# Expert inputs fetched as rows by an indirect DMA instead of computed as one-hot products

## The chip, the cores and the metric

The kernel runs on one core of a Trainium2 chip. The metric is the device time of one execution in microseconds (us). A core has TensorE (PE in the profile; its weight loads are PEld), VectorE (DVE), ScalarE (ACT), GpSimd (POOL) and SyncE (SP), each with an instruction queue of its own that runs in order, and 16 DMA engines that all queues share. SP issues nearly all transfers here; POOL can issue them too, and is the engine that issues an indirect one, whose source addresses come from a table of indices.

## The reference, cut to what matters

A two-layer decoder trunk on 256 tokens of width 1024, float32. The last sub-layer, which takes more than half of the time, is a mixture of 8 SwiGLU experts of which each token uses two:

```python
logits = (ht @ router)                       # 256 x 8
top_logit, top_idx = lax.top_k(logits, 2)
top_w = jax.nn.softmax(top_logit, axis=-1)
xb = h_pad[row_tok]                          # the tokens of an expert, as rows
...
gt, up = jnp.split(xe @ w_gu[e], 2, axis=-1) # w_gu[e]: 1024 x 7168
yb = (jax.nn.silu(gt) * up) @ w_down[e]      # w_down[e]: 3584 x 1024
out = zeros.at[row_tok].add(yb * row_w)
```

512 assignments go to 8 experts, 64 each on average, not all equal. What an expert needs as its input is a selection of the 256 rows of `h`, with the model dimension on the partitions, since that is what TensorE contracts over.

## The kernel before, in words

An expert is worked on in 128 slots. `rank` gives each token its slot in each expert. `slots` (line 1965) makes the one-hot matrix `P` (two tiles of 128 tokens x 128 slots) by comparing `rank` with an iota on DVE. `slots_t` (1973) transposes `P` on PE into `PT`, which later carries the expert's output back to the tokens (`back`, 2055). `disp` (1979) makes the expert's input: for each of eight 128-wide pieces of the model dimension, two float32 products of a piece of `hn` (the 256 rows of `h`, kept in SBUF) with `P` give the piece of the selected rows, already transposed, in PSUM. `disp_out` (1986) splits it into a high and a low float32r part: `xeh` by ACT, `xel` by DVE. `part` (1991) is one third of that: 0 makes and transposes `P`, 1 and 2 make four pieces each.

The weights of all eight experts are streamed once. `wstream` (456) loads tiles of 1 MB (or two halves) into twelve rotating `raw` buffers; of each 512 KB ACT makes the high part (`whi<-raw`) and DVE the low part (`wlo<-raw,whi`), in four rotating pairs, and `mm3` (448) issues three float32r products for each 512 columns: high x high, high x low, low x high. An expert has seven column blocks j. For each, `run_experts` (2184) issues the gate (8 x 3 products of 512 columns), the down projection of the block before (24) and the up projection (24). The next expert's `part`s are hung into the up projection of block 4, behind its products k = 1, 4 and 7 (lines 2197 to 2199).

Up to the routing the order on the engines is set by the kernel's own list of tasks (`spin`). In the expert loop the framework orders the instructions when the kernel is built; for the first experts it keeps the order in which they are written, and from the middle on it interleaves them. A few weight tiles go to buffers that are later used for something else (`raw_once`, 2231), among them `lnbb`, which in the end holds the last layer norm's bias, loaded by `ln_rows` (1484) from `moe_hook` (2219).

SP issues a load when its buffer has been released by DVE. It runs its instructions in order, so a transfer that waits holds back the loads behind it.

Of the kernel before, what the change touches and what calls it, by code (L numbers as in the profile page):

```python
# [24 lines left out]
F32 = mybir.dt.float32  # L25
F32R = mybir.dt.float32r
I32 = mybir.dt.int32
# [5 lines left out]
D = 1024  # L33
S = 256
DFF = 2816
NE = 8
# [4 lines left out]
LNX_EPS = 64e-5  # L41
RANK0 = 1000
NEG = -1.0e30
CW = 1029


def _consts():
    p = np.arange(128)[:, None]
    j = np.arange(128)[None, :]
    c = np.zeros((128, CW), np.float32)  # L50
    c[:, 0:128] = p == j
    c[:, 128:256] = p < j
    c[:, 256:384] = j - RANK0
    c[:, 384:512] = (p <= j) & (p // 64 == j // 64)
    t = j % 64
    s = p % 64
    c[:, 512:640] = np.where(j < 64, s < t, s <= t)
    q = np.arange(64)[None, :]
    c[:, 640:704] = (q % 2 == 1) & (s == q - 1)
    for i, b in enumerate((2, 4, 8, 16)):  # L60
        c[:, 704 + 64 * i:768 + 64 * i] = ((q // b) % 2 == 1) & (s // b == q // b - 1)
    c[:, 960:1024] = s == q
    c[:, 1024] = np.arange(128) == 63
    c[:, 1025] = np.arange(128) == 127
    s = s[:, 0]
    c[:, 1026] = -0.5 * KAPPA * (s + 1)
    c[:, 1027] = 0.5 * KAPPA * (s + 1) - np.log(2.0)
    c[:, 1028] = -0.5 * KAPPA * s
    a = np.zeros((128, 1152 + 256), np.float32)
    for b in range(2):  # L70
        qq = b * 128 + p
        nk = 128 * (b + 1)
        kk = np.arange(nk)[None, :]
        d = qq - kk
        ok = [(d >= 0) & (d <= 128), (d >= 0) & (d % 4 == 0), (d >= 0) & (d % 16 == 0)]
        o = 0 if b == 0 else 384
        for g in range(3):
            a[:, o + g * nk:o + (g + 1) * nk] = np.where(ok[g], 0.0, NEG)
    half = 32
    inv = (np.float32(10000.0) ** (-np.arange(half, dtype=np.float32) / np.float32(half))).astype(np.float32)  # L80
    ang = np.arange(S, dtype=np.float32)[:, None] * inv[None, :]
    cos = np.cos(ang).astype(np.float32)
    sin = np.sin(ang).astype(np.float32)
    for tt in range(2):
        sl = slice(tt * 128, tt * 128 + 128)
        a[:, 1152 + tt * 64:1152 + tt * 64 + 64] = np.concatenate([cos[sl], cos[sl]], 1)
        a[:, 1280 + tt * 64:1280 + tt * 64 + 64] = np.concatenate([-sin[sl], sin[sl]], 1)
    return c, a
# [3 lines left out]
def tile_kernel(ctx: ExitStack, tc: tile.TileContext, cst_d, att_d, x, c, ada_w, ada_b, ln_g, ln_b, mu, w_rkv,  # L92
                w0, w1, w2, a0, a1, a2, g1, g2, k_k, k_a, r_k, lnx_g, lnx_b, w_out, kv_w, w_q, w_o, f_gu, f_dn,
                router, m_gu, m_dn, out):
    nc = tc.nc
    SY = nc.sync
# [30 lines left out]
    class Engine:  # L127


        def __init__(self, real, nm):  # L130
            self.real, self.nm = real, nm
# [62 lines left out]
    V, SC, GP, PE = Engine(nc.vector, "V"), Engine(nc.scalar, "SC"), Engine(nc.gpsimd, "GP"), Engine(nc.tensor, "PE")  # L194
    PSUM = bass.MemoryType.PSUM

    cp = ctx.enter_context(tc.tile_pool(name="cp", bufs=1, reuse_waits="tile"))
# [16 lines left out]
    def pt(j, shape=(128, 512)):  # L214
        return ringed(("pt", j), 1, ps_pool[1].tile(list(shape), F32, name="psb", tag=f"pt{j}"))

    def pst(shape=(128, 512), dt=F32):
        if len(ps_pool) == 1:
            ps_lane[0] = (ps_lane[0] + 1) % 4
            return ps_pool[0].tile(list(shape), dt, name="psb", tag=f"psb{ps_lane[0]}")  # L220
        ps_lane[0] = ps_lane[0] % pst_n[0] + 1
        return pt(4 - ps_lane[0], shape)
# [47 lines left out]
    ident, triS, iota = (cst[:, i:i + 128] for i in (0, 128, 256))  # L270
# [15 lines left out]
    ps = pst((128, 120))  # L286
# [7 lines left out]
    ps = pst((128, 112))  # L294
# [324 lines left out]
    up = rw_stack.enter_context(tc.tile_pool(name="up", bufs=2, reuse_waits="tile"))  # L619
    a_stack = ExitStack()  # L620
    ap_ = a_stack.enter_context(tc.tile_pool(name="ap", bufs=1, reuse_waits="tile"))

    cst2 = up.tile([128, CW - 384], F32, name="cst2", bufs=1)
    SY.dma_start(cst2, cst_d[:, 384:CW])
    triI, smask, lmT1 = cst2[:, 0:128], cst2[:, 128:256], cst2[:, 256:320]
    lmT = {b: cst2[:, 320 + 64 * i:384 + 64 * i] for i, b in enumerate((2, 4, 8, 16))}
    i64, sel = cst2[:, 576:640], cst2[:, 640:642]
# [33 lines left out]
    for t in range(2):  # L661
        for hf in range(2):
            ps = pst((128, 4, 128))
# [194 lines left out]
    rows, rsb, vsb, done = {}, {}, {}, {}  # L858
# [594 lines left out]
    def pick(engines, *aps):  # L1453

        return min(engines, key=lambda e: e.start(aps))
# [22 lines left out]
    pn = ctx.enter_context(tc.tile_pool(name="pn", bufs=1, reuse_waits="tile"))  # L1478
# [31 lines left out]
    for j in range(6):  # L1510
        n = min(512, DFF - j * 512)
# [312 lines left out]
    hn, xtra, raw4 = [], [], []  # L1824
# [109 lines left out]
        yield from pn_res(t, u, pre3["gb"], pre3["bb"], GP)  # L1934

    mdt, mdn, hdone = {}, {}, set()

    def hn_task(t, hf):

        yield lambda: mdn.get(t, 0) > hf and banks.ok()  # L1940
        jt, tmp, _ = mdt[t, hf]
        j, ps = banks.get((128, 4, 128))
        yield PE, tmp
        for i in range(4):
            PE.transpose(ps[:, i], tmp[:, i], ident)
        tmps.put(jt)
        e = pick([SC, V], ps)
        yield e, ps
        (SC.copy if e is SC else V.tensor_copy)(hn[0][:, t, hf * 512:(hf + 1) * 512],
                                                ps.rearrange("p a b -> p (a b)"))  # L1950
        banks.put(j)
        hdone.add((t, hf))


    macc = []
    e_n, ep, late = [0], [], {}

    class Expert:


        def __init__(self, gu, dn, rcol, wcol, first):
            self.gu, self.dn, self.rcol, self.wcol, self.first = gu, dn, rcol, wcol, first
            self.xh = None

        def slots(self):
# [20 lines left out]
        def disp_out(self, hf, ps):  # L1986
            sl = slice(hf * 4, hf * 4 + 4)
            SC.copy(self.xh[:, sl], ps)
            V.tensor_tensor(self.xl[:, sl], ps, self.xh[:, sl].bitcast(F32), op=OP.subtract)

        def part(self, n):
            if n == 0:
                self.slots()
                self.slots_t(pst((128, 2, 128)))
            else:
                ps = pst((128, 4, 128))
                self.disp(n - 1, ps)
                self.disp_out(n - 1, ps)
# [56 lines left out]
        def back(self, t):  # L2055
            for hf in range(2):
# [9 lines left out]
                else:  # L2066
# [5 lines left out]
    route = {nm: pn.tile([128, 2, 8], BF16 if nm == "M" else F32, name=nm) for nm in ("M", "oh1", "Wt", "rank")}  # L2072
# [1 line left out]
    alpha = pn.tile([128, 1], F32, name="alpha")  # L2074
    GP.memset(alpha, ALPHA)
    experts = [Expert(m_gu[0, e], m_dn[0, e], lambda t, e=e: route["rank"][:, t, e:e + 1],
                      lambda t, e=e: route["Wt"][:, t, e:e + 1], e == 0) for e in range(NE)]

    def route_task():

# [97 lines left out]
    Wt, rank, cmaxi = route["Wt"], route["rank"], route["cmaxi"]  # L2178
# [5 lines left out]
    def run_experts(exps, hook=None):  # L2184
        prev = old = None
        if exps[0].xh is None:
            for n in range(3):
                exps[0].part(n)
        for i, e in enumerate(exps):
            for j in range(7):  # L2190
                mg, mu_ = {}, {}
                if prev:
                    mg[1] = [prev[0].tr]
                if old and j == 1:
                    mg[5] = [lambda o=old: o.back(1)]
                nxt = exps[i + 1] if i + 1 < len(exps) else None
                if nxt and j == 4:
                    for n in range(3):
                        mu_.setdefault(1 + 3 * n, []).append(lambda e=nxt, n=n: e.part(n))
                e.gate(j, mg)  # L2200
                if not nxt and j == 6:
                    e.up(j, mu_)
                if prev:
                    prev[0].down(prev[1], [e.tr] if not nxt and j == 6 else ())
                    if prev[1] == 6:
                        old = prev[0]
                        old.fin(False)
                        mu_[5] = [lambda o=old: o.back(0)]
                if nxt or j < 6:
                    e.up(j, mu_)  # L2210
                prev = (e, j)
                if hook and i == len(exps) - 1 and j == 2:
                    hook()
        e.down(6, fine=True)
        e.fin(True)
        for t in range(2):
            e.back(t)
# [9 lines left out]
    def once(pool, tag, bufs=1):  # L2227
# [4 lines left out]
                     14: [once(adap, "acc"), once(pn, "gate1")], 17: [once(pn, "lngb"), once(pn, "lnbb")],  # L2232
                     18: [once(pn, "u", 2), once(pn, "u", 2)]})
    run_experts(experts, moe_hook)


    rank2 = ep[0].tile([128, 2, 8], F32, name="rank2")
    V.tensor_scalar(rank2, rank, -128.0, None, op0=OP.add)
    dtab = ctx.enter_context(tc.tile_pool(name="dtab", bufs=1, space=bass.MemoryType.DRAM))
    tab = dtab.tile([NE, 128, 4], F32, name="tab")  # L2240
    rw8 = ep[0].tile([128, NE, 4], F32, name="rw8")
    V.tensor_copy(rw8[:, :, 0:2], rank2.rearrange("p t e -> p e t"))
# [3 lines left out]
    with tc.If(cv > 128):  # L2246
        with tc.For_i(0, NE, 1) as ei:
            rw1 = ep[0].tile([128, 4], F32, name="rw1")
            SY.dma_start(rw1, tab[bass.ds(ei, 1)].rearrange("e p f -> p (e f)"))
            run_experts([Expert(m_gu[0, bass.ds(ei, 1)].rearrange("e k n -> (e k) n"),  # L2250
                                m_dn[0, bass.ds(ei, 1)].rearrange("e k n -> (e k) n"),
                                lambda t: rw1[:, t:t + 1], lambda t: rw1[:, 2 + t:3 + t], False)])

    gb, bb = late["ln"]
    mvs = []
# [49 lines left out]
```

## Time and profile before

| | us |
|---|---|
| median of three runs | 1827.49 (1825.79 to 1829.19) |
| the profiled execution | 1827.28 |
| its span, first to last instruction | 1825.5 |
| one expert in the first half of the expert loop | 123.6 |
| one expert in its second half | 126.1 to 126.7 |
| PE, busy share of the span | 92% |
| DVE, busy share | 82% |
| ACT, busy share | 62% |
| POOL, busy share | 16% |

The expert loop runs from about 796 us to about 1810 us. POOL has no work in it until 1718 us. What lies around the span in the profiled execution is 1.8 us. A busy PE includes the modelled ends of pipelined products, so what a product costs is read from the distance between two starts, not from its duration.

### The profile page before, as it was taken

The page shows a single profiled execution, that of the slowest core. Times are in us where ns is not written, and L with a number is a line of the kernel's source. Part 1 is how long each engine was busy: PE and PEld are TensorE (multiplying, and loading weights), DVE is VectorE, ACT ScalarE, POOL GpSimd, SP SyncE. Part 2 cuts the span into 40 slices and gives each one's busy share as a digit, 9 for nine tenths or more (in the row PEclk, how much of TensorE's full clock was granted, in tenths as well). Part 3 has the DMA queues.
Part 4 walks back from the last instruction along what each step waited for, and adds up shares of the span by engine and source line. Part 5 has one row for each costly group of instructions (what it writes and reads, how often), then busy time and mean ns, then how long its engine had stood idle before and what let it go on. Part 6 is the DMA issues. An engine that isn't in the chain of part 4 may idle for free. (4 is left out here: it accounts for less than half of the span.)

```text
span 1825.5 us, 26566 instructions
## 1 busy us (share of the span) xinstructions
PE 1687.7 (92%) x9876; PEld 1341.9 (74%) x9876; DVE 1499.5 (82%) x2072; ACT 1136.4 (62%) x1542; POOL 287.9 (16%) x205
## 2 busy tenths in 40 slices
PE   6998888699997888879999999999999999999896
PEld 3686656478885666778888888888788787787784
DVE  2787786789967678579898898988988888988887
ACT  2445444255643656347777777877777777777673
POOL 0011111345414876320000000000000000000200
PEclk8999989799998999989999999999999999999998
DMA  9461551279884765478999999999999999999880
GB/s 333 146 188 62 182 188 36 81 284 334 306 296 143 241 231 177 143 286 303 332 358 374 353 350 355 367 355 338 347 346 359 347 352 348 348 350 342 308 319 25
DMA packets 213565, 498.95 MB, mean 273 GB/s; under 512 B 14634, under 2 KB 28818, under 8 KB 213428
## 3 DMA queue, kind: packets, MB, share of 16 engines
q1 hardware_dynamic: 212564, 494.03, 76.3%
q0 software_dynamic: 864, 3.15, 0.5%
q8 instruction: 79, 1.29, 0.3%
q14 instruction: 58, 0.48, 0.1%
HBM read 496.07 MB, written 1.06 MB: 272 GB/s over the span
## 5 line engine op out<-in xcount | busy, mean ns | idle before, releaser
L191 DVE TENSOR_TENSOR wlo<-raw,whi 128x1024 fp32r<-128x1024 f32 (+1 forms) x799 | 990.3, 1277 | 141.5 <-ACT whi L191 127.4
L191 ACT CAST whi<-raw 128x1024 fp32r<-128x1024 f32 x808 | 823.6, 1047 | 279.8 <-PE mmb L191 209.9
L191 PE MATMUL mmb<-wlo,xeh 128*128 128x512 f32 x896 | 356.6, 398 | 4.7 <-DVE wlo L191 4.0
L191 PE MATMUL mmb<-whi,xeh 128*128 128x512 f32 x896 | 353.4, 395 | 0.0
L191 PE MATMUL mmb<-whi,xel 128*128 128x512 f32 x896 | 352.1, 393 | 0.0
L191 PEld LDWEIGHTS mmb<-wlo,xeh 128*128 128x128 f32 x896 | 168.7, 188 | 46.7 <-DVE wlo L191 13.2
L191 PEld LDWEIGHTS mmb<-whi,xeh 128*128 128x128 f32 x896 | 168.8, 188 | 34.3 <-ACT whi L191 0.2
L191 PEld LDWEIGHTS mmb<-whi,xel 128*128 128x128 f32 x896 | 168.8, 188 | 32.7
L191 PE MATMUL psb<-wlo,ah 128*128 128x512 f32 x448 | 176.7, 394 | 1.5 <-DVE wlo L191 1.5
L191 PE MATMUL psb<-whi,al 128*128 128x512 f32 x448 | 174.9, 390 | 0.0
L191 PE MATMUL psb<-whi,ah 128*128 128x512 f32 x448 | 162.0, 392 | 0.0
L191 POOL TENSOR_TENSOR macc<-macc,gate 128x1024 f32<-128x1024 f32 x2 | 5.7, 2888 | 925.2 <-ACT gate L191 925.2
L191 POOL TENSOR_TENSOR acc<-acc,raw 128x512 f32<-128x512 f32 (+1 forms) x62 | 128.3, 2082 | 72.2 <-DVE acc L191 41.8
L191 PEld LDWEIGHTS psb<-wlo,ah 128*128 128x128 f32 x448 | 84.1, 188 | 24.7 <-DVE wlo L191 6.2
L191 PEld LDWEIGHTS psb<-whi,ah 128*128 128x128 f32 x448 | 83.5, 188 | 18.8 <-ACT whi L191 1.6
L191 PEld LDWEIGHTS psb<-whi,al 128*128 128x128 f32 x448 | 84.2, 188 | 16.4
L191 PE MATMUL mmb<-whi,f_xh 128*128 128x512 f32 (+1 forms) x192 | 74.1, 387 | 3.6 <-ACT f_xh L191 3.6
L191 PE MATMUL mmb<-whi,f_xl 128*128 128x512 f32 (+1 forms) x192 | 73.4, 382 | 1.9 <-DVE f_xl L191 1.9
L191 PE MATMUL mmb<-wlo,f_xh 128*128 128x512 f32 (+1 forms) x192 | 73.4, 382 | 0.2 <-DVE wlo L191 0.2
L191 ACT CAST ah<-psb 128x512 fp32r<-128x512 f32 x56 | 32.6, 583 | 61.0 <-PE psb L191 60.8
L191 ACT ACTIVATE e_s<-mmb 128x512 f32<-128x512 f32 x56 | 33.5, 599 | 44.9 <-PE mmb L191 44.9
L191 DVE TENSOR_TENSOR e_s<-e_s,mmb 128x512 f32<-128x512 f32 x56 | 38.3, 684 | 22.4 <-PE mmb L191 22.2
(429 smaller groups left out, 2559.8 us busy)
## 6 DMA issues: line engine op xcount, KB each, us to landing
raw<-in_moe_w_gu_dram SPq DMA_DIRECT2D x192, 1024.0 KB, 6.9
raw<-in_moe_w_down_dram SPq DMA_DIRECT2D x83, 1024.0 KB, 6.3
raw<-in_moe_w_gu_dram SPq DMA_DIRECT2D x60, 512.0 KB, 7.6
raw<-in_moe_w_down_dram SPq DMA_DIRECT2D x56, 512.0 KB, 6.0
raw<-in_ada_w_dram SPq DMA_DIRECT2D x37, 512.0 KB, 5.0
rawa<-in_ada_w_dram SPq DMA_DIRECT2D x35, 512.0 KB, 4.7
raw<-in_ada_w_dram SPq DMA_DIRECT2D x15, 1024.0 KB, 7.3
raw<-in_ffn_w_gu_dram SPq DMA_DIRECT2D x21, 512.0 KB, 5.6
```

Of the source, the lines that this page charges most:

```text
L191: return fn(*a, **kw)
```

## The change

For every expert but the first the input is no longer made by `disp`. The normalised rows `hn` are also written to a DRAM tile `hrows` (four stores of 256 KB from SP, each behind the copy that makes that quarter of `hn`). `rows` multiplies `P` with a column of token numbers (`tok`, a new constant of two columns) in two float32 products of one column, which gives for each slot the number of its token (0 for an empty slot); DVE casts it to an integer, `ix`; POOL issues an indirect DMA that fetches 128 rows of 4 KB from `hrows` into `xr`, which takes the buffer `lnbb`. `part` 1 and 2 then transpose four 128 x 128 pieces of `xr` each on PE. `part` 0 moves from block 4 to block 3 of the expert before, 1 and 2 stay in block 4.

```diff
@@ hn_task
         banks.put(j)
+        SY.dma_start(hrows[t * 128:(t + 1) * 128, hf * 512:(hf + 1) * 512], hn[0][:, t, hf * 512:(hf + 1) * 512])
         hdone.add((t, hf))
@@ class Expert
+        def rows(self):
+
+            ps = pst()
+            for t in range(2):
+                PE.matmul(ps[:, 0:1], self.P[:, t], tok[:, t:t + 1], start=t == 0, stop=t == 1)
+            ix = ep[0].tile([128, 4], I32, name="ix", tag="rw1")[:, 0:1]
+            V.tensor_copy(ix, ps[:, 0:1])
+            self.xr = pn.tile([128, D], F32, name="xr", tag="lnbb")
+            nc.gpsimd.indirect_dma_start(self.xr, None, hrows, bass.IndirectOffsetOnAxis(ap=ix, axis=0))
+
         def part(self, n):
             if n == 0:
                 self.slots()
                 self.slots_t(pst((128, 2, 128)))
+                if self.e:
+                    self.rows()
+            elif self.e:
+                ps = pst((128, 4, 128))
+                for i in range(4):
+                    PE.transpose(ps[:, i], self.xr[:, (n * 4 + i - 4) * 128:(n * 4 + i - 3) * 128], ident)
+                self.disp_out(n - 1, ps)
             else:
@@ run_experts
-                if nxt and j == 4:
-                    for n in range(3):
+                if nxt and j in (3, 4):
+                    for n in ((0,) if j == 3 else (1, 2)):
                         mu_.setdefault(1 + 3 * n, []).append(lambda e=nxt, n=n: e.part(n))
```

The instructions on the engines move with it. On PE, in the middle of expert 0, where the input of expert 1 is made (`cst` is the identity, `e_s` and `ah` belong to the down projection, `xeh` and `xel` are the current expert's input), before:

```order
L191 MATMUL psb<-cst,P 128x128 x2
L191 MATMUL mmb<-whi,xeh 128x512
L191 MATMUL mmb<-wlo,xeh 128x512
L191 MATMUL mmb<-whi,xel 128x512
L191 MATMUL mmb<-whi,xeh 128x512
L191 MATMUL mmb<-wlo,xeh 128x512
L191 MATMUL mmb<-whi,xel 128x512
L191 MATMUL mmb<-whi,xeh 128x512
L191 MATMUL mmb<-wlo,xeh 128x512
L191 MATMUL mmb<-whi,xel 128x512
L191 MATMUL psb<-P,hn 128x128 x8
L191 MATMUL mmb<-whi,xeh 128x512
```

and now, at the earlier place in block 3 (the eight transposes of `xr` stand, in two groups of four, where the two groups of `P,hn` stood):

```order
L193 MATMUL mmb<-whi,xel 128x512
L193 MATMUL psb<-cst,P 128x128 x2
L193 MATMUL psb<-tok,P 128x1 x2
L193 MATMUL mmb<-whi,xeh 128x512
L193 MATMUL mmb<-wlo,xeh 128x512
```

Between `tok,P` and the first `cst,xr` stand 81 products of 512 columns; for experts 2 and 3 it is the same.

On PE in expert 3, where the input of expert 4 is made, the products with `hn` stood before in six pieces spread over the projections. One of them:

```order
L191 MATMUL psb<-whi,ah 128x512 x2
L191 MATMUL psb<-P,hn 128x128 x3
L191 MATMUL psb<-wlo,ah 128x512
L191 MATMUL psb<-whi,al 128x512
L191 MATMUL psb<-wlo,ah 128x512
L191 MATMUL psb<-whi,al 128x512
```

Now, at `tok,P` and then at the first transposes of `xr`, with seven rows of one product each between the two pieces:

```order
L193 MATMUL mmb<-whi,xeh 128x512
L193 MATMUL psb<-tok,P 128x1 x2
L193 MATMUL mmb<-wlo,xeh 128x512
L193 MATMUL mmb<-whi,xel 128x512
L193 MATMUL mmb<-whi,xeh 128x512
L193 MATMUL mmb<-wlo,xeh 128x512
L193 MATMUL mmb<-whi,xel 128x512
L193 MATMUL psb<-whi,ah 128x512 x2
```

```order
L193 MATMUL psb<-whi,ah 128x512
L193 MATMUL psb<-wlo,ah 128x512
L193 MATMUL psb<-whi,al 128x512
L193 MATMUL psb<-whi,ah 128x512 x2
L193 MATMUL psb<-cst,xr 128x128 x3
L193 MATMUL psb<-wlo,ah 128x512
```

Counted through, 19 products of 512 columns stand between `tok,P` and the first `cst,xr` for experts 4 and 6, and 23 for experts 5 and 7.

On SP, at the end of the routing, the loads of the first expert's weights before:

```order
L119 DMA raw<-in_moe_w_gu_dram 128x4x512 x3
L119 DMA raw<-in_moe_w_gu_dram 128x2x512
L119 DMA raw<-in_moe_w_gu_dram 128x4x512 x4
L119 DMA raw<-in_moe_w_down_dram 128x1024 x2
L119 DMA raw<-in_moe_w_gu_dram 128x2x512
L119 DMA raw<-in_moe_w_gu_dram 128x4x512
```

and now:

```order
L121 DMA raw<-in_moe_w_gu_dram 128x2x512
L1958 DMA hrows<-hn 128x512 x2
L121 DMA raw<-in_moe_w_gu_dram 128x4x512 x2
L1958 DMA hrows<-hn 128x512 x2
L121 DMA raw<-in_moe_w_gu_dram 128x4x512 x2
L121 DMA raw<-in_moe_w_down_dram 128x1024 x2
L121 DMA raw<-in_moe_w_gu_dram 128x2x512
```

The four stores stand between the loads, so six loads now come behind the last of them. The load of the last bias into `lnbb` moves on SP from among the loads of expert 0 to among those of expert 7.

## Rows read from the trace of the kernel before

**Rows 1.** The page: busy time of each engine over the span.

```profile
PE 1687.7 (92%) x9876; PEld 1341.9 (74%) x9876; DVE 1499.5 (82%) x2072; ACT 1136.4 (62%) x1542; POOL 287.9 (16%) x205
```

**Rows 2.** Busy time by stretch, one expert each: first half, second half.

```profile
core 0: us, PE busy (x) PEld busy (x) DVE busy (x) ACT busy (x) POOL busy (x), PEclk, DMA share, GB/s
928.50:1052.10 123.60, 123.60 (x575) 102.23 (x574) 113.26 (x109) 96.77 (x104) 0.00 (x0) 1.00 1.00 359
...
1300.30:1426.40 126.10, 125.63 (x575) 101.75 (x575) 111.18 (x109) 93.57 (x103) 0.00 (x0) 1.00 0.98 350
```

**Rows 3.** Waits of the engines, 820 to 1240 us: total us, times, longest.

```profile
ACT whi L191 <- PE mmb L191: 50.8, 151, 1.2
...
ACT whi L191 <- DMA raw<-in_moe_w_gu_dram: 0.3, 1, 0.3
```

**Rows 4.** Waits of SP's queue, 820 to 1240 us.

```profile
SPq L119 <- DVE wlo L191: 347.3, 163, 6.8
```

**Rows 5.** Busy time by stretch: the refill of the buffers, and the expert loop's first half.

```profile
775.00:797.00 22.00, 11.57 (x68) 11.21 (x69) 19.45 (x51) 4.47 (x10) 13.10 (x8) 0.66 1.04 394
820.00:1240.00 420.00, 420.00 (x1949) 347.09 (x1948) 382.84 (x364) 327.63 (x350) 0.00 (x0) 1.00 0.97 349
```

**Rows 6.** Timeline of PE, 1000 to 1020 us: start, duration, then the instruction.

```profile
1001.61 1.95 PE L191 MATMUL psb<-P,hn 128*128 128x128 f32 x16
1003.31 0.48 PE L191 MATMUL mmb<-whi,xeh 128*128 128x512 f32 x1
...
1008.61 0.60 PE L191 MATMUL psb<-cst,e_s 128*128 128x128 f32 x4
1008.96 0.48 PE L191 MATMUL mmb<-whi,xeh 128*128 128x512 f32 x1
1009.28 0.39 PE L191 MATMUL mmb<-wlo,xeh 128*128 128x512 f32 x1
...
1013.17 0.39 PE L191 MATMUL psb<-whi,ah 128*128 128x512 f32 x1
...
1018.39 0.39 PE L191 MATMUL psb<-whi,al 128*128 128x512 f32 x1
```

**Rows 7.** Line 119 on POOL: the six weight loads of 512 KB it issues.

```profile
L119 POOL DMA_DIRECT2D raw<-in_moe_w_gu_dram x4: 722/742/762, 768.7 to 790.7; - x4
L119 POOL DMA_DIRECT2D raw<-in_moe_w_down_dram x2: 564/638/712, 728.1 to 774.1; - x2
...
DMA to landing us min/median/max: 4.1/7.1/8.2
```

**Rows 8.** Timeline of DVE, 773 to 782 us.

```profile
770.90 8.47 DVE L191 SCALAR_TENSOR_TENSOR ln_a<-ln_y,ln_v 128x1 f32<-128x1 f32 x1
...
781.44 0.15 DVE L191 TENSOR_REDUCE ix<-cnd 128x1 f32<-128x8 f32 x1
```

**Rows 9.** Timeline of POOL, 767 to 800 us.

```profile
769.50 4.68 POOL L191 TENSOR_TENSOR wlo<-raw,whi 128x1024 fp32r<-128x1024 f32 x2
774.12 0.56 POOL L119 DMA_DIRECT2D raw<-in_moe_w_down_dram  x1
774.70 4.64 POOL L191 TENSOR_TENSOR wlo<-raw,whi 128x1024 fp32r<-128x1024 f32 x2
```

**Rows 10.** Busy time by stretch in the last expert, where PE waits; PEclk is third from the end.

```profile
1720.00:1727.40 7.40, 3.63 (x14) 2.04 (x12) 5.89 (x3) 2.20 (x3) 7.40 (x3) 1.00 0.78 272
1727.40:1730.80 3.40, 3.25 (x10) 2.69 (x11) 3.40 (x3) 1.67 (x3) 3.40 (x2) 0.50 0.69 267
```

**Rows 11.** Timeline of PE, 1718 to 1733 us.

```profile
1729.32 0.63 PE L191 MATMUL mmb<-whi,xel 128*128 128x512 f32 x1
1729.74 0.63 PE L191 MATMUL mmb<-whi,xeh 128*128 128x512 f32 x1
1730.17 0.63 PE L191 MATMUL mmb<-wlo,xeh 128*128 128x512 f32 x1
```

**Rows 12.** Timeline of ACT, 765 to 805 us: the last copy that makes hn.

```profile
787.70 0.59 ACT L191 COPY hn<-mmb 128x512 f32<-128x512 f32 x1
```

**Rows 13.** Timeline of SP, 767 to 812 us: weight loads issued.

```profile
771.91 3.09 SPq L119 DMA_DIRECT2D raw<-in_moe_w_gu_dram  x5
775.11 4.51 SPq L119 DMA_DIRECT2D raw<-in_moe_w_down_dram  x2
779.71 1.82 SPq L119 DMA_DIRECT2D raw<-in_moe_w_gu_dram  x2
805.43 4.91 SPq L119 DMA_DIRECT2D raw<-in_moe_w_down_dram  x3
```

More of the change, by code (lines that the diff above doesn't have):

```diff
@@ L43 @@
 NEG = -1.0e30
-CW = 1029
+CW = 1031
 def _consts():
@@ L65, in _consts @@
     s = s[:, 0]
+    c[:, 1029] = np.arange(128)
+    c[:, 1030] = c[:, 1029] + 128
     c[:, 1026] = -0.5 * KAPPA * (s + 1)
@@ L621, in tile_kernel @@
     ap_ = a_stack.enter_context(tc.tile_pool(name="ap", bufs=1, reuse_waits="tile"))
-    cst2 = up.tile([128, CW - 384], F32, name="cst2", bufs=1)
-    SY.dma_start(cst2, cst_d[:, 384:CW])
+    cst2 = up.tile([128, 645], F32, name="cst2", bufs=1)
+    SY.dma_start(cst2, cst_d[:, 384:1029])
     triI, smask, lmT1 = cst2[:, 0:128], cst2[:, 128:256], cst2[:, 256:320]
@@ L1936, in tile_kernel @@
     mdt, mdn, hdone = {}, {}, set()
+    dtab = ctx.enter_context(tc.tile_pool(name="dtab", bufs=1, space=bass.MemoryType.DRAM))
+    hrows = dtab.tile([S, D], F32, name="hrows")
+    tok = cp.tile([128, 2], F32, name="tok")
+    SY.dma_start(tok, cst_d[:, 1029:1031])
     def hn_task(t, hf):
@@ L1958, in tile_kernel, with __init__ @@
     class Expert:
-        def __init__(self, gu, dn, rcol, wcol, first):
-            self.gu, self.dn, self.rcol, self.wcol, self.first = gu, dn, rcol, wcol, first
+        def __init__(self, gu, dn, rcol, wcol, e):
+            self.gu, self.dn, self.rcol, self.wcol, self.e, self.first = gu, dn, rcol, wcol, e, e == 0
             self.xh = None
@@ L2076, in tile_kernel @@
     experts = [Expert(m_gu[0, e], m_dn[0, e], lambda t, e=e: route["rank"][:, t, e:e + 1],
-                      lambda t, e=e: route["Wt"][:, t, e:e + 1], e == 0) for e in range(NE)]
+                      lambda t, e=e: route["Wt"][:, t, e:e + 1], e) for e in range(NE)]
     def route_task():
@@ L2238, in tile_kernel @@
     V.tensor_scalar(rank2, rank, -128.0, None, op0=OP.add)
-    dtab = ctx.enter_context(tc.tile_pool(name="dtab", bufs=1, space=bass.MemoryType.DRAM))
     tab = dtab.tile([NE, 128, 4], F32, name="tab")
@@ L2251, in tile_kernel @@
                                 m_dn[0, bass.ds(ei, 1)].rearrange("e k n -> (e k) n"),
-                                lambda t: rw1[:, t:t + 1], lambda t: rw1[:, 2 + t:3 + t], False)])
+                                lambda t: rw1[:, t:t + 1], lambda t: rw1[:, 2 + t:3 + t], None)])
     gb, bb = late["ln"]
```

## The prediction

> **What bounds the kernel now.** I read the page first: PE is busy 92% of the span and DVE 82% [rows 1]. These are averages over stages, so I went on to the busy time by stretch, one expert at a time: 123.6 us per expert in the first half of the loop with PE busy all of it, 126.1 in the second half with PE busy 125.6 [rows 2]. A DMA share near 1.00 stands in the same rows and looks like a second bound, so the next views were the waits. ACT, which opens the chain that splits the weights, waited 50.8 us for PE to release buffers and 0.3 us for a transfer [rows 3]; SP's queue waited 347 us of 420 for DVE to release the load buffers [rows 4]. The transfers fill what is free: before the loop they ran at 394 GB/s, in it at 349 [rows 5]. So in the loop PE's instruction stream sets the pace, and a microsecond less on PE is a microsecond less in the end as long as nothing makes PE wait. Last I read PE's timeline for prices by the distance of starts: 24 products of 512 columns lie between 1013.17 and 1018.39, thus 5.22 / 23 = 0.227 us each [rows 6].
>
> **What the change removes on PE.** One `disp` (eight float32 products, sixteen instructions in the trace) runs from 1001.61 to the next product at 1003.31: 1.70 us, two per expert, 3.40 us [rows 6].
>
> **What it adds on PE.** Four float32 transposes of 128 columns, those of `e_s`, take 1008.61 to 1008.96, 0.35 us [rows 6]; eight for `xr` are 0.70 us. The two products with `tok` have one column and no row of their own. They cost at least nothing and at most two products with `hn`, 2 x 1.70 / 8 = 0.42; I take 0.2. Each change between float32 and float32r costs the next product some 0.09 us (1009.28 - 1008.96 = 0.32 instead of 0.23) [rows 6]; `tok` adds one such place in the later experts, the fewer pieces take some away, and I leave this at 0, within 1 us over all. Gain per expert 3.40 - 0.70 - 0.20 = 2.5 us, times seven experts **17.5 us**, if the rows of `xr` are there in time.
>
> **When the rows come.** The path from `tok` to `xr` is new: product, cast on DVE, indirect DMA, landing. The casts are as short as the 0.15 us of a one-column DVE instruction [rows 8], and DVE is busy 111 to 113 of 124 to 126 us [rows 2], so seven of them are covered there. With the product's end and the signals I put 0.6 us ahead of POOL. POOL is idle in the loop [rows 2]; nothing stands before the DMA there. Its price is the open one. The nearest rows are POOL's own six loads of the same size, 512 KB: 4.1 us to landing at least, 7.1 median, 8.2 at most, of which POOL spends 0.56 to 0.76 us on the issue [rows 7]. I take the median of the six, 7.1, since most of them went out while the weight stream was running, as it does in the loop, and one more issue of 0.7 us, since here every address comes from a table: 0.6 + 7.1 + 0.7 = **8.4 us**. The lower end is 0.6 + 4.1 = 4.7; the upper one is 0.6 + 8.2 + two more issues, 10.3.
>
> The cover, from the order of the changed kernel: for experts 1 to 3, 81 products of 0.227 us, 18.4 us, more than the upper end, so these gathers are hidden. For experts 4 and 6 it is 19 products, 4.3 us; for 5 and 7 it is 23, 5.2 us. There PE, which runs in order, stands at the first transpose of `xr` with the down and gate projections behind it; ACT's `xeh` cast waits behind the same transposes, with only some two weight tiles split ahead, so nothing is made up afterwards. The waits: 2 x (8.4 - 4.3) + 2 x (8.4 - 5.2) = **14.6 us**, with ends 2 x 0.4 = 0.8 and 2 x 6.0 + 2 x 5.1 = 22.2.
>
> A wait of PE has a second price. In the last expert PE was busy 3.63 of 7.40 us and kept its full clock in that stretch; in the next 3.4 us the granted clock was 0.50, the 1.2 GHz level [rows 10], and products started every 0.43 us instead of 0.227 [rows 11]: 3.4 x (1 - 0.227 / 0.43) = 1.6 us lost. There PE had been idle for 3.8 us in several pieces before the clock fell; the new waits are 3.2 and 4.1 us in one piece. I take 1.6 us for each of the four, **6.4 us**, with 0 and 3.2 each as ends.
>
> A rule of the Trainium skill on the first price: "DMA: Bandwidth & Descriptors", the anatomy of one DMA on the gpsimd path, gives about 2.0 us plus bytes over 436 GB/s, an estimate of 3.2 us for 512 KB by that page. By it no gather would be late and the sum would be the whole gain, 1810 us. The six loads took 4.1 to 8.2 us [rows 7], so the trace doesn't agree, and the sum goes by the rows.
>
> **What else moves.** The four stores stand on SP between weight loads; the last waits until hn's last copy ends at 788.3 [rows 12]. Six loads that SP issued from 773 to 781 us come after it, some 15 us later. What hides this: after 781.5 SP had nothing to issue until 805.4, all buffers being full [rows 13], and the six refill at 394 GB/s [rows 5] in 12 us. Without that cover it would be up to 15 us. The added traffic, 1 MB of stores and seven gathers, is 4.7 MB, 12 us of DMA time that lies in the slack of [rows 4]. `part` 0 moves a block earlier with two compares and an ACT cast that are the same as before. The load into `lnbb` moves to the last expert, where only the final norm needs it. The end of the kernel keeps its length.
>
> **The sum.** Against the profiled execution's own 1827.3 us, 0.2 under the median: -17.5 + 14.6 + 6.4 = +3.5, **1831 us**. By the ends: -17.5 + 0.8 gives 1811; -17.5 + 22.2 + 12.8 gives 1845.
>
> **Rivals.** *The gather is quick.* If it lands as the quickest of POOL's loads did, 4.7 us after `tok`, PE waits 0.8 us in all and the clock holds: 1811 us; at 6 us (waits 5.0 us) it is 1815. From 17.5 / 4 = 4.4 us of loss per late expert, clock included, the change stops paying. For it: the slower of the six stood behind a queue that was being refilled at 394 GB/s [rows 5], denser than the loop. Against: the loop's queue is never empty, share 0.97 [rows 5]. By the page's rule above it would be this case.
>
> *The waits are there, the clock is not lost.* Then -17.5 + 14.6 = -3, 1824 us. For it: PE kept its clock through 3.8 us of waits spread over 7.4 [rows 10], and here each wait is alone. Against: the next stretch lost it.
>
> *POOL is kept from writing the gather's descriptors.* Two-input instructions of DVE and POOL exclude each other: one DVE instruction on a single column took 8.47 us [rows 8] beside POOL's 4.68 and 4.64 us of subtractions [rows 9]. In the loop DVE runs such subtractions nearly all the time; if the indirect DMA needs the same access, once for reading the table and again for writing, a gather takes two DVE instructions longer, 2 x 382.84 / 364 = 2.1 us [rows 5]. Then the four waits grow by 8.4 us, and the sum is +12, 1839 us. The Trainium skill states this lock, in "SBUF — State Buffer", section "SBUF: two separate sides": descriptors for a DMA from POOL wait until the DVE instruction ends. The rows show the lock in the other direction only; whether it holds a DMA of POOL no run here shows.
>
> *The transfers bound instead.* Then the gain is lost and 4.7 MB at 349 GB/s add 13 us, 1840. Against it [rows 4] and the 394 GB/s of [rows 5].
>
> **Chances.** Forecast (gather 7.4 to 9.4 us after `tok`, clock lost at most waits; 1826 to 1836) 0.48, of which 0.18 within the band; quick gather 0.20; waits without the clock 0.14; descriptor lock 0.15; transfers 0.03. Some 0.2% (3.7 us) is what a measurement of this kernel can tell from no change. Faster: the quick gather and 0.03 of the waits without the clock, 0.23. Same: 0.18 + 0.11 = 0.29. Slower: 0.30 + 0.15 + 0.03 = 0.48. The likeliest case alone spans 1826 to 1836; the range that holds 8 in 10 reaches into both sides, 1815 to 1843.
>
> **What would show it.** Right: the matmul groups `psb<-P,hn` are gone but for expert 0; `psb<-cst,xr` waits for the DMA of `xr` four times, 3 to 5 us each, and not in experts 1 to 3; the granted clock falls to 0.5 for a stretch after such waits; expert times are about 121 us in the first half and 128 to 129 in the second (126.1 - 2.5 + 3.7 + 1.6). Wrong: `xr` rows land within 5 us and PE never waits; ACT's `whi` waits for transfers in the loop; SP's loads behind the stores make ACT wait in expert 0; or the first half's experts don't get shorter, which would mean that something other than PE's stream sets their pace.

## The result, and the profile after

The changed kernel takes 1839.1 us (median of five runs, 1838.2 to 1841.5), the kernel before on the same chip 1828.7: a ratio of 1.0057, 95% interval 1.0046 to 1.0069. Forecast were 1831 us in a range of 1815 to 1843, with slower the likeliest. The direction was right, the point 8 us too low, and the span of the likeliest case alone, 1826 to 1836, does not hold the measured time.

The page after, first part, answers to [rows 1]: PE is busy 7 us less in a span that is 11 us longer.

```profile
PE 1680.8 (92%) x9736; PEld 1328.5 (72%) x9736; DVE 1495.9 (81%) x2079; ACT 1133.8 (62%) x1542; POOL 298.0 (16%) x212
```

Next come busy times by stretch, cut where the first product `mmb<-yl,PT` of each expert starts, so that a row has the length of one expert and holds the making of one input. The columns are those of [rows 2]. First the kernel before: the stretches with the inputs of experts 4 and 5, and the end from the last of these products on.

```profile
1180.23:1303.76 123.53, 123.38 (x571) 101.18 (x569) 109.50 (x107) 92.14 (x102) 0.00 (x0) 1.00 0.97 349
1303.76:1429.89 126.13, 125.66 (x575) 101.78 (x574) 111.21 (x109) 93.57 (x104) 0.00 (x0) 1.00 0.98 350
...
1682.82:1825.50 142.68, 119.83 (x527) 94.72 (x525) 121.54 (x136) 83.85 (x93) 12.37 (x4) 0.94 0.60 219
```

The changed kernel, cut at the same products: the input of expert 2, those of experts 4 to 7, and the end.

```profile
930.98:1052.28 121.30, 121.30 (x556) 99.80 (x554) 112.98 (x110) 96.72 (x104) 1.91 (x1) 1.00 1.00 369
...
1172.99:1305.37 132.38, 127.29 (x556) 101.15 (x555) 111.47 (x110) 92.72 (x104) 1.87 (x1) 0.97 0.93 337
1305.37:1433.83 128.46, 125.37 (x556) 100.59 (x555) 111.17 (x110) 93.40 (x104) 0.94 (x1) 0.99 0.96 348
1433.83:1560.84 127.01, 124.44 (x555) 99.24 (x554) 111.08 (x108) 92.77 (x104) 1.69 (x1) 1.00 0.97 350
1560.84:1692.10 131.26, 126.22 (x555) 101.41 (x554) 110.78 (x108) 93.44 (x104) 1.68 (x1) 0.97 0.95 342
1692.10:1836.40 144.30, 119.82 (x527) 94.84 (x525) 119.67 (x136) 83.96 (x93) 11.36 (x4) 0.94 0.60 219
```

The first half gains 2.3 us per expert (123.60 to 121.30 for the input of expert 2; the next row, 120.7 instead of 123.6, ends in a block that only the changed kernel interleaves). The four stretches in which the inputs of experts 4 to 7 are made take 132.4, 128.5, 127.0 and 131.3 us instead of 123.5, 126.1, 126.7 and 126.2: 16.5 us lost. The end is 1.6 us longer. Up to 1173 us the changed kernel is 7.2 us ahead: -7.2 + 16.5 + 1.6 = +10.9, the difference of the spans. One trace stands against one trace here: in five traces of kernels that hardly differ up to there (this one and runs 1, 5, 6 and 9), the first cut lies anywhere between 929.4 and 932.8 us.

The wait is where it was expected. All work on the tile `xr` in the changed kernel, with who waited for it:

```profile
L2006 POOL DMA_INDIRECT xr<-hrows,ix x7: 939/1690/1914, 861.0 to 1610.8; - x7
...
  PE psb L193: 12.7, 4
...
DMA to landing us min/median/max: 5.6/8.4/8.8
```

PE around the longest but one of these waits, for the input of expert 4 (timeline; in brackets the idle time and what ended it):

```profile
1217.27 0.50 PE L193 MATMUL psb<-tok,P 128*128 128x1 f32 x4
1217.63 0.49 PE L193 MATMUL mmb<-wlo,xeh 128*128 128x512 f32 x1
1217.95 0.40 PE L193 MATMUL mmb<-whi,xel 128*128 128x512 f32 x1
...
1226.64 0.90 PE L193 MATMUL psb<-cst,xr 128*128 128x128 f32 x3 [4.23 <-DMA xr<-hrows,ix]
...
1228.19 0.63 PE L193 MATMUL psb<-wlo,ah 128*128 128x512 f32 x1
1228.62 0.63 PE L193 MATMUL psb<-whi,al 128*128 128x512 f32 x1
```

`xr` is used 9.4 us after `tok`; the other three waits are 2.46, 1.64 and 4.42 us long. After it the products start every 0.43 us. The stretches behind the four waits, the third from the end being the granted clock:

```profile
1225.70:1232.50 6.80, 5.86 (x16) 4.69 (x17) 0.00 (x0) 0.02 (x1) 0.00 (x0) 0.50 0.82 325
1362.20:1365.60 3.40, 3.40 (x10) 2.85 (x11) 1.42 (x2) 2.29 (x3) 0.00 (x0) 0.50 1.04 399
1484.70:1488.10 3.40, 3.38 (x17) 2.81 (x18) 1.41 (x2) 0.14 (x1) 0.00 (x0) 1.00 0.99 399
1618.20:1625.00 6.80, 5.61 (x16) 4.55 (x17) 1.92 (x2) 3.42 (x4) 0.00 (x0) 0.50 0.62 241
```

The clock is at its 1.2 GHz level for 6.8, 3.4 and 6.8 us, and keeps 2.4 GHz after the shortest wait. Of these 17 us, 2.2 lie within the waits themselves.

### The profile page after: what moved, and what is told of

It is laid out like the page before. It is cut to its first block, busy times and chain, and to the rows that moved or that the text cites. A ratio compares the mean times of both kernels' runs of the same rounds, so it can differ in the third digit from the quotient of the medians.

```text
span 1836.4 us, 26314 instructions
## 1 busy us (share of the span) xinstructions
PE 1680.8 (92%) x9736; PEld 1328.5 (72%) x9736; DVE 1495.9 (81%) x2079; ACT 1133.8 (62%) x1542; POOL 298.0 (16%) x212
## 5 line engine op out<-in xcount | busy, mean ns | idle before, releaser
L193 PEld LDWEIGHTS mmb<-wlo,xeh 128*128 128x128 f32 x896 | 169.7, 189 | 50.8 <-DVE wlo L193 16.5
L2006 POOL DMA_INDIRECT xr<-hrows,ix x7 | 11.4, 1628 | 807.5 <-DVE ix L193 388.1
```

Of the source, the lines that this page charges most:

```text
L193: return fn(*a, **kw)
L2006: nc.gpsimd.indirect_dma_start(self.xr, None, hrows, bass.IndirectOffsetOnAxis(ap=ix, axis=0))
```

## The experiments

Theory: the late gathers make PE wait and cost it the clock. Rivals: the order or the traffic costs, not the wait; the gather is slow for a reason of its own (one row read many times, the table of addresses, DVE holding POOL up).

**1. No wait.** PE keeps its instructions and their order, but that for experts 5 and 7 the first four transposes stand twelve products earlier. The selection of rows is left out.

```diff
-                    PE.transpose(ps[:, i], self.xr[:, (n * 4 + i - 4) * 128:(n * 4 + i - 3) * 128], ident)
+                    PE.transpose(ps[:, i], hn[0][:, 0, (n * 4 + i - 4) * 128:(n * 4 + i - 3) * 128], ident)
```

> The changed kernel, but the eight transposes per expert read rows 0 to 127 of hn in SBUF where they read xr; the gather is still issued and lands, nobody reads it (so experts 1 to 7 get the wrong tokens). PE's instructions and their order are the same, the wait for the DMA is gone. Theory A (the late experts lose their time to the wait for the gather and to the clock that falls after it): the four gaps of PE, 4.4 + 2.6 + 1.8 + 4.6 = 13.4 us, go, and with them the 17 us at half clock, some 8 us: 1839 - 21 = about 1818 us. Theory B (the interleaved order itself, or the traffic of gather and stores, is what costs): within 3 us of the changed kernel, 1836 to 1839.

Measured: 1820.6 us, 0.9956 of before [0.9941, 0.9971]. The wait and its clock are worth 18.5 us; theory A holds. The same stretches as above in this kernel:

```profile
1174.70:1300.00 125.30, 124.36 (x556) 99.21 (x555) 111.41 (x110) 92.76 (x104) 1.87 (x1) 1.00 0.97 354
1300.00:1424.50 124.50, 123.75 (x555) 99.41 (x554) 111.19 (x110) 93.36 (x104) 0.94 (x1) 1.00 1.00 363
1424.50:1549.73 125.23, 124.29 (x556) 99.34 (x554) 111.05 (x108) 92.79 (x104) 1.69 (x1) 1.00 0.98 357
1549.73:1674.18 124.45, 123.71 (x556) 99.43 (x555) 110.73 (x108) 93.38 (x104) 1.68 (x1) 1.00 0.99 359
```

They sum to 499.5 us, against 519.1 with the wait and 502.6 in the kernel before. So wait and clock cost 19.6 us here, but without them the four late experts gain only 3.1 us, not 10. That gap is the open question for the later runs.

**2. The gather one block earlier.**

```diff
-                if nxt and j in (3, 4):
-                    for n in ((0,) if j == 3 else (1, 2)):
+                if nxt and j in (2 if i else 3, 4):
+                    for n in ((0,) if j < 4 else (1, 2)):
```

> The changed kernel with part 0 of the next expert (slots, their transposes, the index product and the gather) one block earlier still, in block 2, for the inputs of experts 2 to 7; 53 to 153 products stand between tok and the first transpose of xr, 12 us at least. Theory A (the gather is only late): no wait of PE for the DMA of xr, the clock stays, about 1818 us as without any wait. Rival (the gather lands late whenever it is issued beside the weight stream, or part 0 costs more at that place): waits of some us stay, 1825 to 1839.

Measured: 1819.0 us, 0.9953 [0.9939, 0.9967]; no wait of PE for `xr`, landing 6.9 to 9.2 us. The gather was late, not too slow.

**3 and 4. PE in the written order,** in the kernel before and in the changed one.

```diff
-    run_experts(experts, moe_hook)
+    with tc.manual_schedule(engines={mybir.EngineType.PE}):
+        run_experts(experts, moe_hook)
```

> The kernel before, with PE kept in the order in which the expert loop is written, where the framework interleaved down and gate products from block 25 of 56 on. Theory A (the interleaved order costs by itself, because it changes more often between float32 and float32r products and between projections: 126.2 instead of 123.6 us per expert): 24 blocks by 2.6 / 7 = 0.37 us less, 9 us, about 1820 us. Rival (the interleaving hides waits for the split weights that come back in the written order): 1826 us or more.

> The changed kernel with PE in the written order through the whole expert loop: 81 products, 18.4 us, between tok and the first transpose of xr for every expert. Theory A (the loss is the order: it shortens the cover of the gather and begins four blocks earlier than in the kernel before): each expert takes some 121.2 us as the first three do, so 1820 (the kernel before in written order) less 7 x 2.3 = about 1804 us, and no wait for xr. Rival (the late gathers are slow for another reason, or the late experts are slower whatever the order): 1815 us or more.

Measured: 1838.3 us, 1.0056 [1.0043, 1.0070], and 1827.5 us, 0.9992 [0.9982, 1.0003]. Theory A fell in both. One expert of the first half and one of the second, the kernel before in written order:

```profile
1066.12:1191.90 125.78, 124.36 (x575) 102.14 (x574) 113.68 (x109) 96.83 (x104) 0.00 (x0) 1.00 0.96 348
1443.61:1569.48 125.87, 125.87 (x575) 101.81 (x574) 110.93 (x107) 94.36 (x104) 0.00 (x0) 1.00 0.97 353
```

The first half got slower by 2.2 us per expert, and the second half hardly got faster (126.1 to 126.7 before). The first half of the kernel before is thus not quite in the written order: there `cst,e_s` stands, in most blocks, two products of 512 columns later than it is written. In the written order PE waits for DVE at it in five of seven blocks, which makes each of them 0.45 us longer:

```profile
1034.46 0.66 PE L191 MATMUL psb<-cst,e_s 128*128 128x128 f32 x4 [0.28 <-DVE e_s L191]
```

These are waits for `e_s`, not for the split weights that the rival named. So the interleaved order of PE alone is not why a late expert takes 126 us; the orders of ACT and DVE changed with it, and what sets 126 us stays open. Against each other the two show the change with all its gathers covered and no wait for `xr`: 10.8 us gained, of which a late expert brings less (124.77 instead of 125.87) than an early one (123.73 instead of 125.78).

**5 and 6. Which rows, and a plain DMA.**

```diff
-                PE.matmul(ps[:, 0:1], self.P[:, t], tok[:, t:t + 1], start=t == 0, stop=t == 1)
+                PE.matmul(ps[:, 0:1], ident, tok[:, 0:1], start=t == 0, stop=t == 1)
```

> The changed kernel, with the index product fed by the identity instead of P, so that slot p fetches row 2p: 128 different rows (experts 1 to 7 get the wrong tokens). In the changed kernel the slots without a token, about half of the 128, all fetch row 0. Theory A (the landing time is the issue, held up by DVE, and a transfer that shares the DMA engines with the weight stream): landing stays at 5.6 to 8.8 us after the issue, four waits of PE, 1836 to 1841 us. Rival (many reads of the same 4 KB make the gather slow): landing falls by 2 us or more, the waits shrink by 8 us and the time goes to 1825 to 1830.

Measured: 1839.5 us, 1.0070 [1.0053, 1.0087], landing 6.1/7.9/8.5 us. That half of the slots read row 0 costs nothing that shows.

```diff
-            nc.gpsimd.indirect_dma_start(self.xr, None, hrows, bass.IndirectOffsetOnAxis(ap=ix, axis=0))
+            GP.tensor_copy(self.xr[:, 0:1], ix)
+            nc.gpsimd.dma_start(self.xr, hrows[0:128])
```

> The changed kernel, with a plain DMA of rows 0 to 127 of hrows issued by POOL where the indirect one stood; so that it is issued at the same moment, POOL first copies ix into one column of xr, which takes perhaps 0.1 to 1.3 us (experts 1 to 7 get the wrong tokens). Theory A (the table of addresses is a small part of the price; most is the time to the first packet and a transfer beside the weight stream): landing 4 to 8 us after the issue as for POOL's weight loads, waits of PE 8 to 14 us in all, 1830 to 1840 us. Rival (the descriptors from a table are what costs): landing 4 us or less, no wait over 1 us, about 1820 us.

Measured: 1833.4 us, 1.0032 [1.0016, 1.0047]. `xr` in this kernel:

```profile
L2007 POOL DMA_DIRECT2D xr<-hrows x7: 531/531/590, 862.3 to 1608.7; - x7
...
  PE psb L193: 10.6, 4
...
DMA to landing us min/median/max: 3.8/6.7/7.2
```

Theory A holds: the indirect form adds 1.7 us to the median landing (8.4 against 6.7), 1.2 of them in POOL's own instruction (1690 ns against 531). The plain DMA is still late, by 10.6 us in four waits; behind `ix` it began 0.3 to 1.2 us later than the indirect one, because of POOL's copy, 3.0 us in these four, so issued at the same moment it would leave some 8 us of waits (an estimate from these numbers).

**7 and 8. The terms that were put at nothing.** In 7 the kernel before gets the store line of the change's `hn_task` and the tile `hrows`, no more; in 8 this:

```diff
-                if nxt and j == 4:
-                    for n in range(3):
+                if nxt and j in (3, 4):
+                    for n in ((0,) if j == 3 else (1, 2)):
```

> The kernel before with the four stores of hn to DRAM alone; nothing reads them. My step: they hold six weight loads up on SP by some 15 us but SP would have been idle, and 1 MB more traffic lies in slack, so 0: within 2 us of the kernel before, first block of expert 0 unchanged. Rival (the refill of the buffers is late): ACT waits for weights in expert 0, and the time rises by up to 15 us.

> The kernel before with part 0 of the next expert (slots and their transposes) in block 3 instead of block 4, the products with hn kept. My step: 0, within 2 us of the kernel before; interleaving of down and gate products begins at block 25 as before, not at block 21 as in the changed kernel. Rival (the earlier compares and casts disturb DVE and ACT): some tenths of a us per expert, 1830 to 1834.

Measured: the stores 1828.8 us, 1.0006 [0.9996, 1.0016], so nothing that can be told. The move 1830.5 us, 1.0017 [1.0007, 1.0028], more than nothing. In its trace the three late experts take 126.91, 126.87 and 126.71 us, 0.5 us each more than before; the first half is unchanged. What costs the half microsecond is not shown. This execution as a whole, 1827.2 us, was no longer than that of the kernel before, 1827.3; its loop began 1.5 us earlier.

**9. Gathers for experts 1 to 3 alone.**

```diff
-                if self.e:
+                if self.e in (1, 2, 3):
                     self.rows()
-            elif self.e:
+            elif self.e in (1, 2, 3):
```

> The changed kernel, with rows and the gather for experts 1 to 3 alone; experts 4 to 7 make their input by products with hn as before (part 0 in block 3). No late gather is left. Theory (from the pitch of the blocks: the three early gathers gain 2.3 us each, 7.0 us; the down and gate products are interleaved from block 21 instead of 25, which takes back 2.9; part 0 in block 3 costs the late experts 0.4 each; the load into lnbb turns ACT's order in the last expert, 1.7): 1828.4 - 7.0 + 2.9 + 1.6 + 1.7 = about 1827.5 us, and blocks 21 to 27 together longer than in the kernel before by some 3 us. Rival (the earlier interleaving costs nothing and what looked like it was the gather's): 1824.5 or less.

Measured: 1827.3 us, 0.9996 [0.9985, 1.0008], as the sum said. The eight blocks in question, from `cst,e_s` to `cst,e_s`, in the kernel before, then here:

```profile
1166.33:1309.90 143.57, 143.27 (x659) 117.27 (x658) 128.36 (x126) 108.10 (x120) 0.00 (x0) 1.00 0.96 348
```

```profile
1159.48:1305.81 146.33, 145.25 (x660) 116.76 (x659) 128.49 (x127) 108.24 (x121) 0.00 (x0) 1.00 0.96 348
```

Both make the input of expert 4 by products; here 2.8 us go (2.6 beside run 8, where the stretch is 143.70), and the framework begins to interleave at block 21 of 56, not 25. In the order of runs 7 and 8 it begins at block 25 still, in that of run 1 at block 21: it comes with the edits in `rows` and the transposes, not with the stores or the move. The four stretches in which experts 4 to 7 get their input, cut as above, sum to

```profile
sum 507.34, PE 504.26 PEld 407.00 DVE 444.09 ACT 373.02 POOL 0.00; mean PE 126.06 PEld 101.75 DVE 111.02 ACT 93.25 POOL 0.00
```

against 502.6 in the kernel before and 499.5 in run 1. Run 1 interleaves from the same block as this run, so replacing the products by transposes, with no wait, gains 7.9 us there, 2.0 per expert.

**10 to 12. The last expert, the index product, and DVE.** Run 10 puts `xr` of run 2 into another buffer; 11 adds a float32r index product; 12 adds one cast.

```diff
-            self.xr = pn.tile([128, D], F32, name="xr", tag="lnbb")
+            self.xr = pn.tile([128, D], F32, name="xr", tag="gate1")
```

> The kernel with the earlier gather (block 2), with xr in the buffer of gate1 instead of lnbb. The load of the last bias is then back among the loads of expert 0 and ACT's order in the last expert is that of the kernel before (four casts whi ahead of the ah that waits, not two). Theory (that order costs 1.7 us in the last expert): 1819.0 - 1.7 = 1817.3 us, block 52 back from 23.8 to 21.3 us. Rival (the last expert is longer for another reason): 1819 us, block 52 unchanged.

Measured: 1816.1 us, 0.9927 [0.9914, 0.9940]. ACT in the last expert (timeline) in the kernel before, the changed one, and run 10:

```profile
1718.31 3.89 ACT L191 CAST whi<-raw 128x1024 fp32r<-128x1024 f32 x4
1729.13 0.59 ACT L191 CAST ah<-psb 128x512 fp32r<-128x512 f32 x1 [6.93 <-PE psb L191]
```

```profile
1727.60 2.00 ACT L193 CAST whi<-raw 128x1024 fp32r<-128x1024 f32 x2
1737.54 0.59 ACT L193 CAST ah<-psb 128x512 fp32r<-128x512 f32 x1 [7.95 <-PE psb L193]
```

```profile
1706.80 3.89 ACT L193 CAST whi<-raw 128x1024 fp32r<-128x1024 f32 x4
1716.97 0.59 ACT L193 CAST ah<-psb 128x512 fp32r<-128x512 f32 x1 [6.28 <-PE psb L193]
```

With the bias load moved out of expert 0, ACT splits two weight tiles instead of four before it waits for `ah`, and PE then waits 1.6 us for `whi`:

```profile
1739.13 0.49 PE L193 MATMUL mmb<-whi,xeh 128*128 128x512 f32 x1 [1.62 <-ACT whi L193]
```

In the free buffer the order of before is back and the block is 21.31 us long again (21.31 before, 22.97 changed, 23.76 in run 2).

```diff
-                PE.matmul(ps[:, 0:1], self.P[:, t], tok[:, t:t + 1], start=t == 0, stop=t == 1)
+                PE.matmul(ps[:, 0:2], self.Pr[:, t], tokr[:, t], start=t == 0, stop=t == 1)
```

> As the kernel before this one (gather from block 2, xr in gate1), and the index product in float32r (P and the token numbers are whole numbers up to 255), two instructions instead of four per expert. Theory (the index product costs its four float32 instructions of 0.11 us, 0.37 with the last, and a change of format): 0.25 to 0.35 us less per expert, 1.7 to 2.5 us in all, about 1815 us. Rival (PE's stream is no longer what sets the pace): no change, 1817 us.

Measured: 1817.6 us, 0.9940 [0.9927, 0.9953], no gain. Each expert is 0.2 us shorter, but the gather for expert 4 landed 13.7 us after its issue, and PE waited 2.1 us in spite of 53 products of cover. POOL, then DVE, at that gather:

```profile
1207.18 6.61 POOL L2010 DMA_INDIRECT xr<-hrows,ix  x1 [117.36 <-DVE ix L193]
```

```profile
1206.76 0.15 DVE L193 CAST ix<-psb 128x1 int32<-128x1 f32 x1
1206.83 0.47 DVE L193 TENSOR_SCALAR P<-cst,rank 128x128 fp32r<-128x128 f32 x2
1207.22 5.76 DVE L193 TENSOR_TENSOR wlo<-raw,whi 128x1024 fp32r<-128x1024 f32 x5
1214.05 0.69 DVE L193 TENSOR_TENSOR e_s<-e_s,mmb 128x512 f32<-128x512 f32 x1 [1.07 <-PE mmb L193]
```

POOL's instruction ended at 1213.79, 0.81 us after the last of five `wlo` without a gap (1212.98). At the same place in runs 2 and 10, behind the same two compares and ahead of a `wlo`, it took 0.94 us. Why POOL was kept out for so long here (the compares write float32r in this run), and whether it is in every execution, one trace does not show.

```diff
             V.tensor_copy(ix, ps[:, 0:1])
+            V.tensor_copy(self.xl[:, 0:8], ix.to_broadcast([128, 1024]).rearrange("p (a b) -> p a b", b=128))
```

> As the kernel before this one, and DVE gets one more instruction with one input per expert behind the cast ix: ix, read 1024 times, goes to xel, which is overwritten later. It stands directly behind ix (or behind one compare) for experts 1 to 4, 6 and 7, so that no wlo, which has two inputs, runs when POOL begins the indirect DMA; for expert 5 two wlo stand in between. Theory (an instruction of DVE with two inputs keeps POOL from the table: DMA_INDIRECT ended 0.81 us after the end of a wlo in each gather where one was running, and took 6.61 us for expert 4 in the kernel before this one, where five wlo ran without a gap, after which PE waited 2.8 us and lost its clock): POOL's DMA_INDIRECT takes 0.9 to 1.0 us for six experts and 1.7 us or more for expert 5, no PE wait for xr, and about 4 us less, 1813 to 1815 us. Rival (any DVE instruction holds POOL, or the time on POOL depends on something else): 1.4 to 2 us as before in all of them.

Measured: 1814.8 us, 0.9919 [0.9903, 0.9934]. No wait for `xr`, and the stretch with that gather takes 124.8 us instead of 128.0; the sizes on POOL were not as expected. The same gather here, POOL and DVE:

```profile
1204.08 1.34 POOL L2011 DMA_INDIRECT xr<-hrows,ix  x1 [117.92 <-DVE ix L193]
```

```profile
1203.92 0.69 DVE L193 CAST xel<-ix 128x1024 fp32r<-128x1024 int32 x1
```

Five gathers took 1.27 to 1.38 us, not 0.9 to 1.0: the cast itself, which has one input, ended at 1204.61, and POOL 0.81 us later. For experts 1 and 5, where a `wlo` was running, it was 2.04 and 1.87. So an instruction of DVE that runs when POOL begins the indirect DMA holds it up, with two inputs or, as this cast, with one.

## Why the prediction was right, and where it was wrong

| term | forecast | measured |
|---|---|---|
| experts 1 to 3 | -7.5 | -7.2 |
| experts 4 to 7, work of PE without any wait | -10.0 | -3.1 |
| the four waits | +14.6 | +12.7 |
| the clock behind them | +6.4 | +6.9 |
| the end | 0 | +1.6 |
| sum | +3.5 | +10.9 |

The measured clock term is the 19.6 us of run 1 less the waits; it holds the restart after a wait as well. It agrees with the prediction's own price: the clock was low for 14.9 us outside the waits, 14.9 x (1 - 0.227 / 0.43) = 7.0.

**Right.** PE's stream sets the pace, the gathers of experts 1 to 3 are hidden, those of 4 to 7 are late by the order of the changed kernel, and their waits and the clock behind them cost 19.6 us where 21.0 was forecast: the four gathers came 9.4, 8.5, 6.6 and 10.3 us after `tok`, 8.7 in the mean where 8.4 was taken from POOL's own loads [rows 7]. By the Trainium skill, "DMA: Bandwidth & Descriptors", anatomy of one DMA, an estimate of 3.2 us had stood against this; no gather in any run landed in less than 5.2 us. The cost put at nothing for the stores was nothing that could be told (run 7); the traffic of the gathers was tested by no run alone.

**Luck.** The two sums are nearer than their parts. Experts 4 and 6 were to wait 4.1 us and 5 and 7 3.2, with "3 to 5 us each" as the sign; the waits were 4.2 and 1.6, and 2.5 and 4.4. In the mean the gather took 0.3 us more than forecast, but PE had 5.5 us of cover where 4.75 was counted. The clock was to fall for 3.4 us behind each wait; it fell for 6.8, 3.4, 0 and 6.8.

**Wrong: the sum took the gain of 2.5 us for all seven experts.** It is 2.3 in the first half. For the late four it is 0.8, and three things stand in its place. The interleaving began four blocks earlier: 2.6 us (run 9). It stood in the instruction order of the changed kernel, and the prediction counted only the products between `tok` and `xr` there. Which of the orders that change with it costs this, PE's, ACT's or DVE's, stays open (runs 3 and 4). Moving `part` 0 was put at nothing and costs 0.5 us per late expert, some 2 us (run 8, which shows three of the four). The rest is 2.3 us over four experts. About 1 us of it is the index product: four float32 instructions take 0.36 us (1217.27 to 1217.63) and the change of format behind them 0.09 more, where 0.20 was taken for the one and nothing for the other. For the other 1.3 no run names a cause; some 0.6 of it may be only the place of the cut behind expert 3's input. The price of `disp` is no part of it. In spread pieces its 32 instructions take 2.9 to 3.1 us by the distances of starts, not 3.40 [rows 6], but each of six to eight pieces is followed by a change of format, so that with these it takes 3.6 us in either form. The largest piece in expert 3, before:

```profile
1253.83 1.05 PE L191 MATMUL psb<-P,hn 128*128 128x128 f32 x8
1254.63 0.48 PE L191 MATMUL mmb<-whi,xeh 128*128 128x512 f32 x1
1254.95 0.40 PE L191 MATMUL mmb<-wlo,xeh 128*128 128x512 f32 x1
```

**Wrong: "The end of the kernel keeps its length".** The load into `lnbb` was put at nothing because only the final norm needs it. It turned ACT's order in the last expert, 1.6 us (run 10).

**The rivals.** The quick gather, waits without loss of clock, and a bound by transfers did not come. The lock of POOL had the time that was measured, 1839 us, but by another sum: it put 2.1 us on each gather and 8.4 on the waits, which then would be 23.0 us and were 12.7. The lock is there, at up to 1.1 us in the changed kernel (DMA_INDIRECT 0.94 to 1.91 us), inside the 8.4 us. The Trainium skill, "SBUF — State Buffer", section "SBUF: two separate sides", has an instruction of DVE keep POOL from writing descriptors until it ends if it runs in a 2-port mode (one that also takes the port pair it shares with POOL); one with two inputs in SBUF keeps out only a POOL instruction that reads SBUF, a condition that the prediction left out. Runs 6, 11 and 12 fit this: the indirect DMA, which has a table to read, ended 0.81 us behind the end of a `wlo` or of the cast, and the plain one did not wait for a `wlo`. Whether the cast ran in a 2-port mode no trace shows.

**A version that beats both:** run 12, and run 10 close to it (intervals overlap): the change with the gather a block earlier and `xr` in a buffer whose last load keeps its place, 0.9919 and 0.9927 of the time before.

## What to carry to other kernels

A transfer that replaces computation is worth its gain only where the cover between issue and first use is longer than the landing time measured under the running load; count that cover in the final order of instructions at each place, since a scheduler may not keep it. Read the rest of that order too: new instructions for one task moved the point where the scheduler interleaves, and one load that changed its place turned another engine's order. When a wait on the engine that sets the pace is priced, add the clock behind it: here 12.7 us of waits cost 19.6.

## What had not been expected of the hardware

- The indirect DMA holds POOL for 0.94 to 2.04 us, ending 0.81 to 0.93 us after the DVE instruction that ran when it began, and once for 6.61 us, over five `wlo`s without a gap (run 11). A plain DMA on POOL took 0.53 to 0.59 us (run 6), though a `wlo` was running when six of the seven began; one of them, POOL and then DVE:

```profile
1353.61 0.53 POOL L2007 DMA_DIRECT2D xr<-hrows  x1 [0.30 <-POOL xr L193]
```

```profile
1353.37 2.35 DVE L193 TENSOR_TENSOR wlo<-raw,whi 128x1024 fp32r<-128x1024 f32 x2
```

- The clock does not follow the length of the wait alone. In the changed kernel it fell after 2.46 us at the input of expert 5, and in run 5 after 2.16 at that of expert 6; in run 6 PE waited 2.86 us for the input of expert 5 and kept 2.4 GHz, here the wait and the stretch behind it:

```profile
1360.52 0.63 PE L193 MATMUL psb<-cst,xr 128*128 128x128 f32 x4 [2.86 <-DMA xr<-hrows]
```

```profile
1361.80:1365.20 3.40, 3.27 (x15) 2.36 (x14) 3.14 (x4) 2.81 (x3) 0.00 (x0) 1.00 0.66 255
```
